# First layer of a two-layer decoder trunk: x read by features for twelve of sixteen tiles, and the fourth gate block of head 0 moved into the first pass

## The chip, the cores and the metric

The kernel runs on one core of a Trainium2 chip. A time is the device time of one launch in microseconds (us). The kernel before takes 2194.3 us, the median of three runs (2192.89 to 2194.66). PE is the matrix engine, DVE the vector engine, ACT the scalar engine, POOL the GpSimd engine, SP the engine that issues most of the DMAs (transfers between device memory and the on-chip memory, SBUF). Products are summed in PSUM, eight banks of 128 x 512 float32.

## The reference, cut to what matters

```python
# D_MODEL 2048, SEQ 512, 2 layers; layer 0: retention (8 heads), layer 1: latent attention
c_act = jax.nn.silu(c)
for i in range(DEPTH):
    mod = (c_act @ ada_w[i] + ada_b[i])[:, None, :]
    shift, scale, gate = jnp.split(mod, 3, axis=-1)
    h = rmsnorm(x, norm_g[i]) * (1.0 + scale) + shift
    ...
    x = x + gate * y
return rmsnorm(x, final_norm_g)

def retention_branch(h, pos, w_in, gn_g, w_out):
    proj = h @ w_in                       # 2048 -> 12288 columns
    q, k, v, g = jnp.split(proj, [RET_QK, 2 * RET_QK, 2 * RET_QK + RET_WIDTH], axis=-1)
    q, k = rope(q), rope(k) * (RET_DK ** -0.5)
    y = groupnorm(chunkwise_retention(q, k, v)) * gn_g
    return (jax.nn.silu(g) * y) @ w_out
```

All is in float32. rmsnorm divides every token (row of x) by its root mean square: one factor per token.

## The kernel before, in words

**Arithmetic.** A float32 operand is split in a high part (rounded to the type that PE multiplies quickly) and a low part (the rest), and a product is three products: high by high, high by low, low by high. ACT casts the high part, DVE subtracts to get the low part.

**Layout.** h is needed by features: 16 tiles hT of 128 features by 512 tokens. x is read by tokens into eight tiles `xs`. `transpose` (L493) turns one feature tile with four 128-wide matmuls against diagonals that hold the token factors, so that x is transposed and normalised at once, into a PSUM bank of the tag `aux`; ACT copies it to `xT` (L502). Six tiles are turned at the start, ten later among the products. `make_first` (L363) takes a finished tile to h: two DVE instructions write one column of shift (`b_col`, L366) and of scale (`a_col`, L367), then ACT writes hT's high half (L243) and a full copy (L245), and DVE subtracts the low half (L246).

**Modulation.** Shift and scale of 128 features need 2 x 1 MB of ada_w (`aw`, four buffers), each multiplied and summed along its rows by one DVE instruction of 2048 elements (`sum_mod`, L353).

**First pass.** The first stage works in eight units of two feature tiles (`for u in range(1, NU)`; unit 0 is written out). As a feature tile of h becomes ready, it is multiplied with three sets of weights of head 0: qk (four 128-row blocks in four PSUM banks `acc`), v (four) and g (three blocks, 384 columns, in three `aux` banks; the transposes use the fourth). qk and v share the four acc banks: `swap` (L373) copies the sums of one set to SBUF (L379) and those of the other back (L383), eight ACT copies in each unit. In the order of a unit on PE: the set that is in the banks ("here", 24 products), g (18), after the swap the other set ("there", 24), and in units 1 to 4 one tile turned after "here" and one after "there".

What the engines do beside unit u is the preparation of unit u+1, `prepare_ahead` (L517) and `prepare_behind` (L535). DVE: sum, low half of the unit's second hT, low half of the "here" weights, sum, columns, sum, low half of hT, low half of g, sum, columns, low half of "there". ACT: cast of "here", hT and its copy, casts of g and "there", the eight copies, second hT. Raw weights have three buffers (`raw`), their high and low parts three each (`whi`, `wlo`); `load_unit` (L506) issues a unit's DMAs on SP. Every engine works in program order; the helper `queued` keeps each piece behind the last instruction already issued on ACT, DVE, PE and SP (not POOL).

**After the first pass.** In unit 7 DVE computes the sine and cosine tables (L257 to L277), whose input `ret_pi` is read by a DMA that ACT issues (L254); ACT takes the sines (L279, L280) and POOL stores both tables (L597). Then a list `steps` of steps (L851) follows: two steps of 24 products each for g's fourth block ("g03", L851, in the free aux bank), and for each further head eight steps of 24 products for qk, then sixteen for v and g together, which use sums and differences of hT's halves (`form_sums`, L626: six DVE additions, two ACT casts, two DVE subtractions for two feature tiles). The steps of g03 form sums 0 and 1 beside their products, the steps of head 1's qk sums 2 to 7. ACT writes the finished banks of head 0 out after the tables and after the cast of the first step's weights (`keep_rows`, L608), and head 1's qk takes over those acc banks one by one. Outputs are stored by DMAs that POOL issues (L612).

`load_residual` (L1138) reads x by features again at the end of the first layer.

Of the kernel before, what the change touches and what calls it, by code (L numbers as in the profile page):

```python
# [9 lines left out]
F32 = mybir.dt.float32  # L10
F32R = mybir.dt.float32r
I32 = mybir.dt.int32
AF = mybir.ActivationFunctionType
ALU = mybir.AluOpType
AX = mybir.AxisListType

P = 128
# [32 lines left out]
def hybrid_trunk_kernel(  # L50
# [44 lines left out]
    def big(name, dt=F32R):  # L95
        return base.tile([P, 2, T], dt, tag="big", bufs=16, name=name)
# [7 lines left out]
    def tmp(name, shape=(P, T)):  # L104
        return base.tile(list(shape), F32, tag="tmp", bufs=6, name=name)
# [4 lines left out]
    def aux(name):  # L110
        return psum.tile([P, T], F32, tag="aux", bufs=4, name=name)
# [22 lines left out]
    def split(src, hi, lo):  # L134
        ACT.copy(hi, src)  # L135
        DVE.tensor_sub(lo, src, hi.bitcast(F32))  # L136
# [16 lines left out]
    def rows(w, u, n, c0, cn):  # L153
        return w[u * n * P : (u + 1) * n * P, c0 : c0 + cn].rearrange("(k p) n -> p k n", p=P)
# [46 lines left out]
    def w_block(w, ki, b):  # L201
        return w[0][:, ki, b * P : (b + 1) * P], w[1][:, ki, b * P : (b + 1) * P]
# [4 lines left out]
    def act_row(t):  # L207
        return t[:, 0, :], t[:, 1, :]
# [89 lines left out]
    def qk_parts(h, u):  # L298
# [10 lines left out]

    first_sets = {  # L310
        "qk": (4, lambda w, kt, b: (w_block(w, kt % 2, b), act_row(hT[kt]))),
        "g": (3, lambda w, kt, b: (w_block(w, kt % 2, b), act_row(hT[kt]))),
        "v": (4, lambda w, kt, b: (act_block(hT[kt], b), w_row(w, kt % 2))),
    }
    banks = {}
# [2 lines left out]

    def first_load(kind, u):

        cn = 384 if kind == "g" else 512
        tags = (("k4b", 4), ("k4b", 4)) if kind == "g" else (("whi", 3), ("wlo", 3))
        raw = base.tile([P, 2, cn], F32, tag="raw", bufs=3, name=f"{kind}0_{u}_raw")
        c0 = {"v": 4096, "g": 8192}.get(kind)
        for dst, src in qk_parts(0, u) if kind == "qk" else [(whole, rows(w_ret_in, u, 2, c0, cn))]:
            nc.sync.dma_start(dst(raw), src)

        def prepare():
            hl = [base.tile([P, 2, cn], F32R, tag=t, bufs=n, name=f"{kind}0_{u}_{t}{i}") for i, (t, n) in enumerate(tags)]
            ACT.copy(hl[0], raw)  # L330
            loaded[kind, u] = hl
            return lambda: DVE.tensor_sub(hl[1], raw, hl[0].bitcast(F32))

        return prepare
# [28 lines left out]
    def make_first(kt):  # L363

        k1 = slice(kt, kt + 1)
        DVE.tensor_add(b_col[0][:, k1], mods[kt, 0], bias_c[0][:, k1])  # L366
        DVE.scalar_tensor_tensor(  # L367
            out=a_col[0][:, k1], in0=mods[kt, 1], scalar=bias1[:, k1], in1=norm_c[0][:, k1], op0=ALU.add, op1=ALU.mult
        )
        hT[kt] = big(f"hT_{kt}")  # L370
        return make_h(0, kt, xT[kt // 2][:, kt % 2, :], hT[kt])
# [48 lines left out]
    def queued(fn, *args):  # L420
        with behind(A_, V_, T_, S_):
            return fn(*args)


    xs = [[big(f"x_{t}_{j}", F32) for j in range(2)] for t in range(NT)]
# [7 lines left out]
    def load_first(kind, u):  # L433
        prepares[kind, u] = queued(first_load, kind, u)

    def load_mods(kt):
        for s in range(2):
            mods[kt, s] = queued(load_mod, kt, s)
# [62 lines left out]
            )  # L501
        return lambda: ACT.copy(xT[kt // 2][:, kt % 2, :], ps)  # L502

    for kt in range(6):
        queued(queued(transpose, kt))
    def load_unit(u):  # L506
        here, there = ("qk", "v") if u % 2 == 0 else ("v", "qk")
        load_first(here, u)
        load_mods(2 * u)
        load_first("g", u)  # L510
        mods[2 * u + 1, 0] = queued(load_mod, 2 * u + 1, 0)
        load_first(there, u)
        mods[2 * u + 1, 1] = queued(load_mod, 2 * u + 1, 1)

    late = {}

    def prepare_ahead(u, first=None):  # L517


        here, there = ("qk", "v") if u % 2 == 0 else ("v", "qk")  # L520
        low = queued(prepares[here, u])
        queued(sum_mod, 2 * u, 0)
        if first is not None:
            queued(first)
        queued(low)
        queued(sum_mod, 2 * u, 1)
        low = queued(make_first, 2 * u)
        queued(sum_mod, 2 * u + 1, 0)
        queued(low)
        low = queued(prepares["g", u])  # L530
        late[u] = queued(prepares[there, u])
        queued(low)
        queued(sum_mod, 2 * u + 1, 1)
# [11 lines left out]
    low = queued(make_first, 0)  # L545
    queued(sum_mod, 1, 0)
    queued(low)
    lows = [queued(prepares[kind, 0]) for kind in ("g", "qk")]
    for low in lows:
        queued(low)  # L550
    queued(sum_mod, 1, 1)
    swap(None, "v")
    queued(products, "v", 0)
    banks["g"] = [aux(f"g0_{b}") for b in range(3)]
    queued(products, "g", 0)
    queued(swap, "v", "qk")
    low = queued(make_first, 1)
    queued(products, "qk", 0)
    prepare_ahead(1, low)
    queued(products, "qk", 1)  # L560
    queued(queued(transpose, 6))
    queued(products, "g", 1)
    queued(swap, "qk", "v")
    low = prepare_behind(1)
    queued(queued(transpose, 7))
    queued(products, "v", 1)
    for u in range(1, NU):

        here, there = ("qk", "v") if u % 2 == 0 else ("v", "qk")
        more = u + 1 < NU  # L570
        ahead = [2 * u + 6, 2 * u + 7] if 2 * u + 7 < KD else []
        if more:
            load_unit(u + 1)
            prepare_ahead(u + 1, low)
        else:
            queued(low)
            for _ in range(8):
                queued(next, tables)
        for kt in (2 * u, 2 * u + 1):
            queued(products, here, kt)  # L580
        for kt in ahead[:1]:
            queued(queued(transpose, kt))
        for kt in (2 * u, 2 * u + 1):
            queued(products, "g", kt)
        if more:
            queued(swap, here, there)
            low = prepare_behind(u + 1)
        else:
            for b, ps in enumerate(banks["v"]):
                st = tmp(f"v0_st{b}")  # L590
                queued(ACT.copy, st, ps)
                POOL.dma_start(v_d[b * P : (b + 1) * P, :], st)
            queued(swap, None, "qk")
            for _ in tables:
                pass
            for n, t in enumerate(ret_tables):
                POOL.dma_start(tables_d[n * P : (n + 1) * P, :], t)  # L597
        queued(bank_products, there, u)
        for kt in ahead[1:]:
            queued(queued(transpose, kt))  # L600
    qk0, g0 = banks["qk"], banks["g"]
    l0.__exit__(None, None, None)

# [4 lines left out]
    def keep_rows(ps, dst_d, r0, name, func=AF.Identity, own=None):  # L608

        st = lpp.tile([P, T], F32, tag="st", bufs=2, name=name) if own is None else own(name)  # L610
        ACT.activation(st, ps, func)
        POOL.dma_start(dst_d[r0 : r0 + P, :], st)  # L612

    H = T // 2

    def sums_tile(n, more):
        shape = [P, 2, 2, H]
        if n < 8:  # L620
            return base.tile(shape, F32R, tag="k4", bufs=8, name=f"sums_{n}")
        if n < 12:
            return base.tile(shape, F32R, tag="k4b", bufs=4, name=f"sums_{n}")
        return more(shape, f"sums_{n}")

    def form_sums(u, acts, sums, staged, more):  # L626
        e, o = (tmp(f"h_{2 * u + i}_f") for i in range(2))
        for f, kt in ((e, 2 * u), (o, 2 * u + 1)):
            DVE.tensor_add(f, acts[kt][:, 0, :].bitcast(F32), acts[kt][:, 1, :].bitcast(F32))
        f = staged(f"sums_{u}_f")  # L630
        DVE.tensor_add(f[0][:, 0, :], e[:, H:], o[:, H:])
        DVE.tensor_sub(f[0][:, 1, :], f[0][:, 0, :], e[:, :H])
        DVE.tensor_sub(f[1][:, 0, :], e[:, :H], e[:, H:])
        DVE.tensor_sub(f[1][:, 1, :], o[:, :H], f[0][:, 1, :])
        for i in range(2):
            s = sums[2 * u + i] = sums_tile(2 * u + i, more)
            split(f[i], s[:, :, 0, :], s[:, :, 1, :])

    def form(acts, sums, n, u, b):

# [188 lines left out]
            lambda second, u: int(second and (u % 2 == 1 or (h > 4 and u > 0))),  # L829
        )  # L830

    sums1, sums2 = {}, {}
    turns1 = turns(
        ((lambda: lpp, "own_r", 3), (lambda: base, "raw", 3)),
        ((lambda: lpp, ("own_h", "own_l"), 1), *3 * ((lambda: base, ("whi", "wlo"), 3),)),
# [12 lines left out]
    def in_turn(i):  # L848
        return None if i % 2 else tmp

    steps = plain_steps(  # L851
        2, 8, lambda u: [(whole, rows(w_ret_in, u, 8, 8192 + 384, P))], P, "g03", aux, 1,
        lambda w, ki, kt, b: w_block(w, ki, b), lambda w, ki, kt, b: act_row(hT[kt]),
        lambda b, ps: keep_rows(ps, g_d, 3 * P, "g0_st3", AF.Silu), sums=lambda u: u,
    )
    for h in range(1, RH):
        if h < 6:
            steps += plain_steps(
# [279 lines left out]
    def load_residual(r, b, tag):  # L1138
        o1_res[b, r] = l1_tile(tag, 4, f"o1_xr{r}_{b}")
        kt = 4 * r + b  # L1140
        nc.sync.dma_start(o1_res[b, r], x_t[kt * P : (kt + 1) * P, :])

    def x1_out(r, b, half=None):

# [749 lines left out]
    n_prepared = prepare_for(0)  # L1894
    for b in range(4):
        queued(keep_rows, qk0[b], qk_d, b * P, f"qk0_st{b}", AF.Identity, in_turn(b))
    for b in range(3):
        queued(keep_rows, g0[b], g_d, b * P, f"g0_st{b}", AF.Silu, tmp)
    for i, step in enumerate(steps):
        if i == n_p:  # L1900
# [272 lines left out]
```

## Time and profile before

| | us |
|---|---|
| median of three runs | 2194.3 |
| the profiled execution | 2192.7 |
| its span on the core | 2190.9 |
| PE busy in the span | 2160.2 |
| DVE busy in the span | 1557.4 |
| ACT busy in the span | 1013.1 |
| POOL busy in the span | 102.5 |
| first unit's products start on PE | 26.16 |
| second unit's products start (chain of waits) | 66.09 |
| g03 starts on PE | 161.64 |
| head 1's qk starts on PE | 173.43 |

The span is from the first to the last instruction on the core, and the profiled execution took 1.8 us more than it. A row of the timeline has the start, the duration, the engine, the line of the kernel, the operation, output and inputs, shapes and a count, and in brackets how long the engine had been idle before and what ended that. A row of the windows has, for one stretch, each engine's busy time (and instructions), the clock granted to PE (1.00 is full speed), the share of the 16 DMA engines that was busy, and the GB/s that they moved.

### The profile page before, as it was taken

How to read it: one execution, taken by the hardware profiler on the slowest of the kernel's cores; microseconds unless marked ns; L12 is line 12 of the kernel's file. 1: busy time of each engine (PE TensorE's matmuls, PEld its weight loads, DVE VectorE, ACT ScalarE, POOL GpSimd, SP SyncE). 2: the span in 40 equal slices, each digit the busy share in tenths (PEclk: the TensorE clock that was granted, in tenths of full speed). 3: DMA queues.
4: the chain of work that ended last, by engine and by line, in shares of the span. 5: the costliest groups of instructions: out<-in, count | busy, mean ns of one | idle time of the engine just before them, and what ended most of it. 6: DMA issues, size and time to landing. Idle time of an engine off the chain costs nothing.

```text
span 2190.9 us, 27827 instructions
## 1 busy us (share of the span) xinstructions
PE 2160.2 (99%) x10280; PEld 1805.1 (82%) x10280; DVE 1557.4 (71%) x2345; ACT 1013.1 (46%) x1529; POOL 102.5 (5%) x178
## 2 busy tenths in 40 slices
PE   7999999999999999999999999999999999999997
PEld 5887888888888878888888888898788889888887
DVE  7878867676676788756677767667877677776545
ACT  5664434434343444434344545344444366664443
POOL 0000000000000000010000000010000000000000
PEclk9999999999999999999999999999999999999998
DMA  9965785867768678574645556453458723235323
GB/s 382 346 246 166 231 295 181 271 214 238 247 197 278 220 256 293 184 244 150 229 156 210 171 190 203 146 161 115 156 192 301 266 87 99 83 113 178 115 99 133
DMA packets 206907, 440.26 MB, mean 201 GB/s; under 512 B 19329, under 2 KB 60321, under 8 KB 202929
## 3 DMA queue, kind: packets, MB, share of 16 engines
q1 hardware_dynamic: 194560, 399.30, 54.7%
q0 software_dynamic: 11920, 38.91, 4.5%
q8 instruction: 80, 1.31, 0.2%
q14 instruction: 57, 0.47, 0.1%
q10 hardware_dynamic: 290, 0.27, 0.0%
HBM read 395.42 MB, written 43.00 MB: 200 GB/s over the span
## 4 chain that ended last, share of the span: by engine, by line
PE 81%; DVE 6%; issue 6%; ACT 3%; DMA 3%; POOL 0%; SPq 0%; POOLq 0%; DVEq 0%; ACTq 0%
PE o L1183 13%; PE qk L163 4%; PE qk L161 4%; PE qk L162 4%; PE o L2039 4%; PE x L729 2%; PE y L729 2%; PE y L730 2%; PE y L728 2%; PE x L730 2%; PE s L729 2%; PE s L730 2%; PE x L728 2%; PE s L728 2%; PE o L162 2%
## 5 line engine op out<-in xcount | busy, mean ns | idle before, releaser
L1183 PE MATMUL o<-o_h,o_whi 128*128 128x512 f32 (+1 forms) x496 | 192.2, 388 | 0.0
L1183 PE MATMUL o<-o_h,o_wlo 128*128 128x512 f32 (+1 forms) x496 | 191.4, 386 | 0.0
L1183 PE MATMUL o<-o_l,o_whi 128*128 128x512 f32 (+1 forms) x496 | 191.3, 386 | 0.0
L163 PE MATMUL qk<-hT,qk_l 128*128 128x512 f32 x448 | 174.9, 390 | 0.5 <-DVE qk_l L136 0.5
L161 PE MATMUL qk<-hT,qk_h 128*128 128x512 f32 x448 | 174.6, 390 | 0.0
L162 PE MATMUL qk<-hT,qk_h 128*128 128x512 f32 x448 | 174.4, 389 | 0.0
L136 DVE TENSOR_TENSOR o_wlo<-o_r,o_whi 128x1024 fp32r<-128x1024 f32 x61 | 74.6, 1223 | 84.1 <-ACT o_whi L135 84.1
L136 DVE TENSOR_TENSOR qk_l<-qk_r,qk_h 128x1024 fp32r<-128x1024 f32 x56 | 68.1, 1224 | 63.7 <-ACT qk_h L135 63.7
L1183 PEld LDWEIGHTS o<-o_h,o_wlo 128*128 128x128 f32 x496 | 93.2, 188 | 18.7
L1183 PEld LDWEIGHTS o<-o_l,o_whi 128*128 128x128 f32 x496 | 93.2, 188 | 18.3
L1183 PEld LDWEIGHTS o<-o_h,o_whi 128*128 128x128 f32 x496 | 93.2, 188 | 18.3
L163 PEld LDWEIGHTS qk<-hT,qk_l 128*128 128x128 f32 x448 | 84.1, 188 | 19.6 <-DVE qk_l L136 2.1
L162 PEld LDWEIGHTS qk<-hT,qk_h 128*128 128x128 f32 x448 | 84.1, 188 | 17.5
L161 PEld LDWEIGHTS qk<-hT,qk_h 128*128 128x128 f32 x448 | 84.1, 188 | 17.4
L135 ACT CAST qk_h<-qk_r 128x1024 fp32r<-128x1024 f32 x56 | 58.0, 1051 | 85.5 <-PE qk L162 62.0
L161 PE MATMUL g<-h,g_h 128*128 128x512 f32 x232 | 90.6, 390 | 0.3 <-ACT g_h L135 0.3
L162 PE MATMUL g<-h,g_h 128*128 128x512 f32 x232 | 90.3, 389 | 0.0
L885 DVE SCALAR_TENSOR_TENSOR mod<-mod,c_bm 128x1024 f32<-128x1024 f32 x64 | 78.1, 1220 | 16.6 <-DMA mod<-in_ada_t_dram 16.5
L163 PE MATMUL g<-h,g_l 128*128 128x512 f32 x232 | 89.8, 389 | 0.0
L353 DVE SCALAR_TENSOR_TENSOR aw<-aw,c_all 128x2048 f32<-128x2048 f32 (+1 forms) x34 | 73.3, 2161 | 2.8 <-DMA aw<-in_ada_t_dram 2.8
L135 ACT CAST o_whi<-o_r 128x1024 fp32r<-128x1024 f32 x61 | 63.6, 1054 | 23.5 <-issue 10.0
L136 DVE TENSOR_TENSOR o_w_lo<-o_w_raw,o_w_hi 128x1024 fp32r<-128x1024 f32 x32 | 39.0, 1221 | 36.7 <-ACT o_w_hi L135 36.6
(1261 smaller groups left out, 6028.4 us busy)
## 6 DMA issues: line engine op xcount, KB each, us to landing
mod<-in_ada_t_dram SPq DMA_DIRECT2D x128, 512.0 KB, 5.8
o_r<-in_ret_w_out_dram SPq DMA_DIRECT2D x64, 512.0 KB, 4.3
aw<-in_ada_t_dram SPq DMA_DIRECT2D x30, 1024.0 KB, 9.0
qk_r<-in_ret_w_in_dram SPq DMA_DIRECT2D x112, 256.0 KB, 4.1
g_r<-in_mla_w_in_dram SPq DMA_DIRECT2D x32, 512.0 KB, 4.4
o_w_raw<-in_mla_w_out_dram SPq DMA_DIRECT2D x32, 512.0 KB, 3.6
qk_d<-qk_st POOLq DMA_DIRECT2D x32, 256.0 KB, 3.7
qk_r<-qk_d SPq DMA_DIRECT2D x32, 256.0 KB, 5.8
```

The lines of the kernel that those rows point to most:

```text
L135: ACT.copy(hi, src)
L136: DVE.tensor_sub(lo, src, hi.bitcast(F32))
L161: PE.matmul(o, lhs[0], rhs[0], start=first and not seeded, stop=False, skip_group_check=seeded)
L162: PE.matmul(o, lhs[0], rhs[1], start=False, stop=False, skip_group_check=seeded)
L163: return PE.matmul(o, lhs[1], rhs[0], start=False, stop=last, skip_group_check=seeded)
L353: DVE.scalar_tensor_tensor(out=aw[:, cols], in0=aw[:, cols], scalar=1.0, in1=c_all[:, cols], op0=ALU.mult, op1=ALU.mult, accum_out=col[:, ...
L728: PE.matmul(banks[b], a[0], w[0], start=first, stop=False, skip_group_check=True)
L729: PE.matmul(banks[b], a[0], w[1], start=False, stop=False, skip_group_check=True)
L730: PE.matmul(banks[b], a[1], w[0], start=False, stop=True, skip_group_check=True)
L885: DVE.scalar_tensor_tensor(out=aw, in0=aw, scalar=1.0, in1=silu_c[j], op0=ALU.mult, op1=ALU.mult, accum_out=mc[:, j, b : b + 1],)
L1183: PE.matmul(o, w[i][:, ki, c0 + b * P : c0 + (b + 1) * P], a[j], start=first and i + j == 0, stop=last and i == 1, skip_group_check=True,)
L2039: PE.matmul(banks2[b][:, cols], w[0][i][:, 0, b * P : (b + 1) * P], o2_moving(w, u, cols)[j], start=u + i + j == 0, stop=u == KD - 1 and i ...
```

## The change

- x is stored by features as pairs of tiles, and tiles 4 to 15 are read by six DMAs of 512 KB, one in each of units 2 to 7, straight into `xT`. Tiles 0 to 3 are still turned on PE. Four more 128-wide matmuls against `ones` spread the token factors over the partitions, ACT copies them to `x_factors`, and one DVE multiplication of 128 x 1024 for each pair (`normalise`) applies them. On DVE it stands between the low half of "here" and the unit's second sum.
- g is multiplied in four blocks (512 columns, four aux banks) in the first pass: 24 products of g in each unit. The two steps g03 are gone, and the list starts with head 1's qk.
- The two columns of `make_first` are written by POOL.
- The raw weights of unit 0 lie in `big` buffers, not in `raw`.
- Sums 0 and 1 are formed in unit 7, on DVE and ACT ahead of the tables.
- `load_residual` reads the new layout of x.

```diff
     first_sets = {
-        "g": (3, lambda w, kt, b: (w_block(w, kt % 2, b), act_row(hT[kt]))),
+        "g": (4, lambda w, kt, b: (w_block(w, kt % 2, b), act_row(hT[kt]))),
...
-        cn = 384 if kind == "g" else 512
+        cn = 512
         tags = (("k4b", 4), ("k4b", 4)) if kind == "g" else (("whi", 3), ("wlo", 3))
-        raw = base.tile([P, 2, cn], F32, tag="raw", bufs=3, name=f"{kind}0_{u}_raw")
+        raw = big(f"{kind}0_{u}_raw", F32) if u == 0 else base.tile(
+            [P, 2, cn], F32, tag="raw", bufs=3, name=f"{kind}0_{u}_raw"
+        )
...
-        DVE.tensor_add(b_col[0][:, k1], mods[kt, 0], bias_c[0][:, k1])
-        DVE.scalar_tensor_tensor(
-            out=a_col[0][:, k1], in0=mods[kt, 1], scalar=bias1[:, k1], in1=norm_c[0][:, k1], op0=ALU.add, op1=ALU.mult
+        POOL.tensor_add(b_col[0][:, k1], mods[kt, 0], bias_c[0][:, k1])
+        POOL.tensor_scalar(
+            out=a_col[0][:, k1], in0=mods[kt, 1], scalar1=bias1[:, k1], scalar2=norm_c[0][:, k1], op0=ALU.add, op1=ALU.mult
         )
...
-    for kt in range(6):
+    for kt in range(4):
         queued(queued(transpose, kt))
+    x_r = aux("x_r")
+    for t in range(NT):
+        queued(PE.matmul, x_r[:, t * P : (t + 1) * P], ones, diags[t], True, True)
+    factors = tmp("x_factors")
+
+    def normalise(u):
+        DVE.tensor_mul(xT[u], xT[u], factors.unsqueeze(1).to_broadcast([P, 2, T]))
+
     def load_unit(u):
...
         load_mods(2 * u)
+        if u > 1:
+            queued(nc.sync.dma_start, xT[u], x_t[u])
         load_first("g", u)
...
         queued(low)
+        if u > 1:
+            queued(normalise, u)
         queued(sum_mod, 2 * u, 1)
...
     queued(low)
+    queued(ACT.copy, factors, x_r)
     lows = [queued(prepares[kind, 0]) for kind in ("g", "qk")]
...
-    banks["g"] = [aux(f"g0_{b}") for b in range(3)]
+    banks["g"] = [aux(f"g0_{b}") for b in range(4)]
...
-    queued(queued(transpose, 6))
...
-    queued(queued(transpose, 7))
...
-        ahead = [2 * u + 6, 2 * u + 7] if 2 * u + 7 < KD else []
...
             queued(low)
+            for n in range(2):
+                queued(form_sums, n, hT, sums1, staged0, None)
             for _ in range(8):
                 queued(next, tables)
...
-        for kt in ahead[:1]:
-            queued(queued(transpose, kt))
...
-        for kt in ahead[1:]:
-            queued(queued(transpose, kt))
...
-    steps = plain_steps(
-        2, 8, lambda u: [(whole, rows(w_ret_in, u, 8, 8192 + 384, P))], P, "g03", aux, 1,
...
-    )
+    steps = []
...
-        nc.sync.dma_start(o1_res[b, r], x_t[kt * P : (kt + 1) * P, :])
+        nc.sync.dma_start(o1_res[b, r], x_t[kt // 2, :, kt % 2, :])
...
-    for b in range(3):
+    for b in range(4):
         queued(keep_rows, g0[b], g_d, b * P, f"g0_st{b}", AF.Silu, tmp)
```

`form_sums` and `sums_tile` are moved ahead of the first pass unchanged.

More of the change, by code (lines that the diff above doesn't have):

```diff
@@ L422, in queued, with sums_tile, form_sums @@
             return fn(*args)
+    H = T // 2
+    def sums_tile(n, more):
+        shape = [P, 2, 2, H]
+        if n < 8:
+            return base.tile(shape, F32R, tag="k4", bufs=8, name=f"sums_{n}")
+        if n < 12:
+            return base.tile(shape, F32R, tag="k4b", bufs=4, name=f"sums_{n}")
+        return more(shape, f"sums_{n}")
+    def form_sums(u, acts, sums, staged, more):
+        e, o = (tmp(f"h_{2 * u + i}_f") for i in range(2))
+        for f, kt in ((e, 2 * u), (o, 2 * u + 1)):
+            DVE.tensor_add(f, acts[kt][:, 0, :].bitcast(F32), acts[kt][:, 1, :].bitcast(F32))
+        f = staged(f"sums_{u}_f")
+        DVE.tensor_add(f[0][:, 0, :], e[:, H:], o[:, H:])
+        DVE.tensor_sub(f[0][:, 1, :], f[0][:, 0, :], e[:, :H])
+        DVE.tensor_sub(f[1][:, 0, :], e[:, :H], e[:, H:])
+        DVE.tensor_sub(f[1][:, 1, :], o[:, :H], f[0][:, 1, :])
+        for i in range(2):
+            s = sums[2 * u + i] = sums_tile(2 * u + i, more)
+            split(f[i], s[:, :, 0, :], s[:, :, 1, :])
     xs = [[big(f"x_{t}_{j}", F32) for j in range(2)] for t in range(NT)]
@@ L515, in hybrid_trunk_kernel, with staged0 @@
     late = {}
+    sums1 = {}
+    def staged0(name):
+        f = l0p.tile([P, D], F32, tag="aw", bufs=4, name=name)[:, 0 : 4 * H].rearrange("p (a n) -> p a n", a=4)
+        return f[:, 0:2, :], f[:, 2:4, :]
     def prepare_ahead(u, first=None):
@@ L612, in keep_rows @@
         POOL.dma_start(dst_d[r0 : r0 + P, :], st)
[L616 to L637, printed above, removed]
     def form(acts, sums, n, u, b):
@@ L830, in heads_steps @@
         )
-    sums1, sums2 = {}, {}
+    sums2 = {}
     turns1 = turns(
@@ L849, in in_turn @@
         return None if i % 2 else tmp
-    steps = plain_steps(
-        2, 8, lambda u: [(whole, rows(w_ret_in, u, 8, 8192 + 384, P))], P, "g03", aux, 1,
-        lambda w, ki, kt, b: w_block(w, ki, b), lambda w, ki, kt, b: act_row(hT[kt]),
-        lambda b, ps: keep_rows(ps, g_d, 3 * P, "g0_st3", AF.Silu), sums=lambda u: u,
-    )
+    steps = []
     for h in range(1, RH):
@@ L2152 @@
     named += [("const_rot_dram", rot), ("const_decay_dram", dec)]
-    named += [("in_x_t_dram", _np.ascontiguousarray(inputs["x"][0].T))]
+    named += [("in_x_t_dram", _np.ascontiguousarray(inputs["x"][0].T.reshape(KD // 2, 2, P, T).transpose(0, 2, 1, 3)))]
     named += [("in_ada_t_dram", _np.ascontiguousarray(_np.swapaxes(inputs["ada_w"], 1, 2)))]
```

## The prediction

> **What bounds the kernel now.** First the page, then the windows, the chain of waits in order of time, and each engine's timeline.
>
> ```profile
> PE 2160.2 (99%) x10280; PEld 1805.1 (82%) x10280; DVE 1557.4 (71%) x2345; ACT 1013.1 (46%) x1529; POOL 102.5 (5%) x178
> ```
>
> PE is the bound of the whole: what the change takes from PE's program counts only where PE is also the last to be ready. So I read the first 180 us by stages.
>
> ```profile
> 30.00:40.00 10.00, 9.73 (x47) 7.70 (x45) 8.73 (x12) 3.88 (x7) 0.00 (x0) 1.00 1.03 403
> 40.00:50.00 10.00, 6.75 (x26) 5.31 (x27) 9.43 (x10) 9.60 (x17) 0.00 (x0) 0.83 1.03 405
> 100.00:110.00 10.00, 10.00 (x50) 8.35 (x49) 8.73 (x10) 6.18 (x10) 0.00 (x0) 1.00 0.86 296
> ```
>
> Up to about 58 us the DMA engines are full (share 1.03 at 405 GB/s) and PE waits once; from then on PE is full, DVE nearly so.
>
> ```profile
> 59.46 5.74 PE qk L396 x24
> 65.20 0.89 PE xT_ps L497 x8
> 66.09 5.46 PE qk L396 x24
> 72.44 4.10 PE g L396 x18
> ```
>
> 24 products take 5.45 us, 18 take 4.10, a turned tile (eight matmul records) 0.89; unit 2 starts at 66.09. A unit of 66 products and two tiles is 16.8 us; without tiles (units 5 to 7) 15.0.
>
> **What paces a unit beside PE.** Unit 6 prepares unit 7; its rows on ACT, DVE and PE, sorted by time:
>
> ```profile
> 131.90 1.06 ACT L330 CAST v_whi<-v_raw 128x1024 fp32r<-128x1024 f32 x1 [0.64 <-PE qk L396]
> 132.99 1.23 DVE L332 TENSOR_TENSOR v_wlo<-v_raw,v_whi 128x1024 fp32r<-128x1024 f32 x1 [1.00 <-ACT v_whi L330]
> 134.13 2.29 DVE L353 SCALAR_TENSOR_TENSOR aw<-aw,c_all 128x2048 f32<-128x2048 f32 x1
> 136.34 0.15 DVE L366 TENSOR_TENSOR b_col<-mc,vcol 128x1 f32<-128x1 f32 x1
> 136.72 0.82 ACT L243 ACTIVATE hT<-xT,b_col,a_col 128x512 fp32r<-128x512 f32 x1 [3.76 <-DVE a_col L367]
> 137.14 4.24 PE L396 MATMUL g<-hT,g_k4b 128*128 128x512 f32 x18
> 138.15 0.82 ACT L330 CAST g_k4b<-g_raw 128x768 fp32r<-128x768 f32 x1
> 138.88 1.05 ACT L330 CAST qk_whi<-qk_raw 128x1024 fp32r<-128x1024 f32 x1
> 140.44 0.59 ACT L383 COPY v<-part_v 128x512 f32<-128x512 f32 x1
> 141.22 0.40 PE L396 MATMUL v<-v_whi,hT 128*128 128x512 f32 x1
> ```
>
> The cast of "here" waits for PE's end of the unit before (its buffer), so the chain starts anew with each unit. The unit starts at about 131.6 (137.14 less 24 products). Chain: cast, low half, sum, columns, hT, cast of g, cast of "there", swap; its first copy ends at 141.03, 9.4 after the start, and PE, done with g at 141.2, takes over without waiting. The chain is just covered, and the tables behind the first pass are too:
>
> ```profile
> 146.25 0.69 DVE L246 TENSOR_TENSOR hT<-h_15f,hT 128x512 fp32r<-128x512 f32 x1 [2.28 <-ACT h_15f L245]
> 144.18 0.36 ACTq L254 DMA_DIRECT2D ret_pi<-in_positions_dram  x1
> 148.31 0.43 DVE L257 CAST ret_sin<-ret_pi 128x512 f32<-128x512 int32 x1 [1.37 <-DMA ret_pi<-in_positions_dram]
> 158.74 0.63 ACT L279 ACTIVATE ret_sin<-ret_sin 128x512 f32<-128x512 f32 x1 [3.00 <-DVE ret_cos L277]
> 159.90 1.04 ACT L135 CAST g_h<-g_r 128x1024 fp32r<-128x1024 f32 x1
> 161.64 0.39 PE L161 MATMUL g<-hT,g_h 128*128 128x512 f32 x1
> 163.02 1.58 ACT L611 ACTIVATE qk_st<-qk 128x512 f32<-128x512 f32 x3 [1.60 <-DMA tables_d<-ret_cos]
> 164.47 1.60 ACT L611 ACTIVATE g_st<-g 128x512 f32<-128x512 f32 x3
> 165.91 1.09 ACT L135 CAST g_h<-g_r 128x1024 fp32r<-128x1024 f32 x1
> 168.18 1.29 DVE L629 TENSOR_TENSOR h_f<-hT 128x512 f32<-128x512 f32 x2
> 170.63 0.43 DVE L634 TENSOR_TENSOR sums_f<-h_f,sums_f 128x256 f32<-128x256 f32 x1
> 171.28 1.29 DVE L136 TENSOR_TENSOR sums<-sums_f,sums 128x512 fp32r<-128x512 f32 x2 [0.23 <-ACT sums L135]
> 173.43 0.39 PE L161 MATMUL qk<-hT,qk_h 128*128 128x512 f32 x1
> 178.96 1.23 DVE L136 TENSOR_TENSOR qk_l<-qk_r,qk_h 128x1024 fp32r<-128x1024 f32 x1 [0.66 <-ACT qk_h L135]
> ```
>
> Unit 7 starts at 146.7 (141.22 plus 5.45) and ends at 161.64. ACT is held by the sines until 159.90 and by the store of the tables until 163.02. PE does not mind: g03 needs neither an acc bank nor those copies, and fills 161.64 to 173.43.
>
> **The change part by part.** PE's own program: twelve tiles less, 12 x 0.89 = 10.7, eight records for the factors more, 0.9; g's 48 products only move. Alone that is -9.8 us. What becomes of it:
>
> (a) *Up to unit 2.* Two raw g blocks grow by 131 KB each, 0.26 MB or 0.65 us at 405 GB/s, ahead of a cast that waits for its DMA:
>
> ```profile
> 41.62 1.05 ACT L330 CAST qk_whi<-qk_raw 128x1024 fp32r<-128x1024 f32 x1 [0.18 <-DMA qk_raw<-in_ret_w_in_dram]
> 43.20 2.07 PE L497 MATMUL xT_ps<-x_diag,x 128*128 128x128 f32 x8 [3.47 <-ACT xT L502]
> ```
>
> The two turned tiles that stood there go (2.07 and 0.89), six products of g come (1.4), and ACT loses a 0.5 us copy behind the cast. At the start hT's first cast falls behind three other ACT pieces in the built order (some 2.3 us), which the 3.47 us of waiting absorb. Unit 2's load is 0.65 MB larger (1.6 us), which its own waits partly show. I take unit 2 at 66.5, +0.4; bounds -1 (loads not later) and +5.7 (two holds as in (b), 2.3 each, beside 1.1).
>
> (b) *Units 2 to 6.* PE's part is 72 products, 16.4 us, against 16.8 or 15.0. The chain grows. `normalise` is one two-input DVE instruction of 1024, 1.14 from the row at 132.99 to the next. The g cast takes 0.23 more (1.05 against 0.82). Then the columns on POOL: before, hT starts 0.38 after the sum's end (136.34). No row shows POOL adding one column; a memset of one column takes 0.10, a power of one column 0.56:
>
> ```profile
> L2149 POOL MEMSET const-float32-0.0<- 128x1 f32 x1 | 0.1, 99 | 0.2 <-issue 0.2
> L131 POOL TENSOR_TENSOR x_r<-x_v,mhalf 128x1 f32<-128x1 f32 x4 | 2.2, 562 | 10.9 <-DVE x_v L129 10.9
> L131 POOL TENSOR_TENSOR gn_r<-gn_v,mhalf 128x4 f32<-128x4 f32 x8 | 8.1, 1015 | 374.0 <-DVE gn_v L129 374.0
> L131 POOL TENSOR_TENSOR kv_r_r<-kv_r_v,mhalf 128x4 f32<-128x4 f32 x1 | 1.9, 1915 | 4.1 <-DVE kv_r_v L129 4.1
> 1657.10 1.22 DVE L885 SCALAR_TENSOR_TENSOR mod<-mod,c_k4b 128x1024 f32<-128x1024 f32 x1
> 1657.28 1.94 POOL L131 TENSOR_TENSOR q_r_r<-q_r_v,mhalf 128x4 f32<-128x4 f32 x1 [75.98 <-DVE q_r_v L129]
> ```
>
> I take 0.4, nearer to the power. The last rows matter more. The same four-column power takes 1.01 eight times, but 1.94 and 1.92 where DVE had just begun a SCALAR_TENSOR_TENSOR with two inputs in SBUF: it ends 0.9 to 1.0 after that instruction's end (1658.32), as if it began there. In the changed order the scale column is released by a sum, and DVE's next instruction is the next sum, of the same kind, 2.21 long, with its data already there. So POOL is held for that sum: hT starts 2.21 + 0.4 + 0.05 = 2.7 after the sum, 2.3 later than before. (With nothing held it would be 0.1 to 0.3 later.) The shift column is not on the path, nor the second scale column, which ACT's copies cover.
>
> [...]
>
> The chain is then 9.4 + 1.14 + 0.23 + 2.3 = 13.1 against 10.9 of products ahead of the swap. PE waits 2.2 us in each unit, and a unit takes 13.1 + 5.45 + 0.15 = 18.7. Five units are 93.5 against 80.6 (66.09 to 146.7): **+12.9**. Without the hold the chain is about 11.0, a unit 16.5, and the five +1.9. DMAs are no bound at this pace: 6.3 MB in 18.7 us are 337 GB/s, under the 405 shown.
>
> (c) *Unit 7 to the steps of head 1's qk.* Counting from unit 7's start: hT's last low half ends at +0.2. Sums 0 and 1 now stand ahead of the tables on DVE, 4.3 each (168.18 to 172.5), and their casts ahead of ret_pi's DMA on ACT. The fourth cast is released at 4.5 + 2.9 = +7.4; the DMA goes then, arrives 4.1 later (144.18 to 148.31), the tables take 10.4 (to 158.74): sines at +22.0. Behind these on ACT come the cast of head 1's first weights, +23.2 (1.16 after the sines' start), the first copy of a qk bank, +24.1, the other three at +26.3 (163.02, 4.3 after the sines' start), four of g to +29.7, and the second weights' cast, so that their low half starts at +30.8. PE is through with unit 7 at +16.4 and waits until +24.7 for a bank: the 10.9 us that g03 took go into this wait. Before, that low half starts at 178.96, +32.3. From there sums, casts and products stand in one order in both: **-1.5**, of which I give 0.5 back for PE's clock, which the window 40 to 50 shows at 0.83 after 3.5 us of waiting. So -1.0; bounds -1.6 (no loss) and +1 (clock lost for longer).
>
> The larger g tiles on DVE (0.27 a unit), the saved tile copies on ACT and load_residual's layout (rows of 2 KB as before) are off these chains: 0, and if the first's cover went, 2 us in all.
>
> Sum: +0.4 + 12.9 - 1.0 = **+12.3**. The profiled execution of before took 2192.7 (span 2190.9 and 1.8), 1.6 under the median of 2194.3; 2205.0 on it is 2206.6 on the median.
>
> **Rivals.** *POOL is not held* (it reads its column in a gap, or DVE's next sum waits for its DMA as at the start): +0.4 + 1.9 - 1.0 = +1.3, 2195.6. For it: only two rows show the hold. Against: DVE has no gaps there. *PE stays the bound* (faster): the point is the place of ret_pi and of the sines on ACT. Were ret_pi's DMA issued ahead of the casts and the first weights cast ahead of the sines, PE would run on at +16.4, and if POOL were also not held the whole 9.8 would be kept: 2184.5. Against: both engines work in program order, and the built order has them as in (c). *PE also loses its clock in each wait*: the trace shows the loss after a wait of 3.5 us, and has no row for one of 2.2. About 1.6 us a unit and five units: +8, 2214.6. [...]
>
> **Chances.** Forecast 0.66 (2200 to 2211: the hold missing in one or two units, or two more at the start); not held 0.17 (2193 to 2198); PE's clock too 0.10; PE the bound 0.05; the change not doing what it says, for x read by features late, 0.02 (DMA again the bound, some 2203). The range 2194 to 2214 leaves out most of the third, the fourth and a part of the second. This kernel's runs differ by 0.1%, so 0.2% (4.4 us) is what can be told from no change: faster 0.05, same 0.18, slower 0.77.
>
> **What would show it.** In the new profile: POOL's a_col at 2.3 to 2.7 us rather than 0.4; ACT's hT waiting for POOL and PE's first product of "there" for ACT's copy, 2 us in each of units 2 to 6; unit starts 18.7 apart; the sines 22 after unit 7's start, and PE waiting 8 us for qk_st ahead of head 1's qk. POOL rows of 0.6 or less, with units 16.5 apart, would prove (b) wrong; a qk that starts before the sines, (c).

## The result, and the profile after

The changed kernel takes **2212.35 us** (median of four, 2210.5 to 2213.3), the kernel before on the same chip 2194.48. The ratio is 1.0082, with a 95% interval from 1.0064 to 1.0099: slower by 0.8%, 17.9 us, where 12.3 were forecast. The profiled execution has a span of 2208.7 against 2190.9, and the first line of its page reads:

```profile
PE 2159.7 (98%) x10192; PEld 1802.5 (82%) x10192; DVE 1560.8 (71%) x2317; ACT 1006.0 (46%) x1516; POOL 140.7 (6%) x210
```

PE has 88 records less, 9.8 us of work by the forecast's count, and is as busy as before (2160.2): some 9.3 us went into running slowly (the mean granted clock is 0.992 against 0.997), and PE's idle time has grown by 18.3 us (49.0 against 30.7). POOL's busy time has grown by 38 us, for 32 columns. PE's timeline shows where PE waits; in brackets stand the length and the releaser.

```profile
62.84 0.50 PE L398 MATMUL qk<-hT,qk_whi 128*128 128x512 f32 x1 [2.32 <-ACT qk L385]
...
73.86 5.60 PE L398 MATMUL g<-hT,g_k4b 128*128 128x512 f32 x24
81.80 0.50 PE L398 MATMUL v<-v_whi,hT 128*128 128x512 f32 x1 [2.34 <-ACT v L385]
...
101.89 0.50 PE L398 MATMUL qk<-hT,qk_whi 128*128 128x512 f32 x1 [1.83 <-ACT qk L385]
...
121.96 0.50 PE L398 MATMUL v<-v_whi,hT 128*128 128x512 f32 x1 [1.83 <-ACT v L385]
...
140.91 0.79 PE L398 MATMUL qk<-hT,qk_whi 128*128 128x512 f32 x1 [2.33 <-ACT qk L385]
...
160.93 0.50 PE L398 MATMUL v<-v_whi,hT 128*128 128x512 f32 x1 [1.83 <-ACT v L385]
...
173.55 5.60 PE L398 MATMUL g<-hT,g_k4b 128*128 128x512 f32 x24
...
190.30 0.79 PE L161 MATMUL qk<-hT,qk_h 128*128 128x512 f32 x1 [5.70 <-ACT qk_st L653]
...
236.39 0.39 PE L745 MATMUL z<-vg_00o_h,hT 128*128 128x512 f32 x1
```

PE waits once in each of units 1 to 6 for ACT's copies of the swap, and once ahead of head 1's qk. A unit's start is the start of its g less 24 products (5.45): unit 2 starts at 68.4, unit 7 at 168.1. The first product of head 1's v and g, at 236.39, stood in the kernel before at

```profile
218.59 0.39 PE L728 MATMUL z<-vg_00o_h,hT 128*128 128x512 f32 x1
```

so the whole 17.8 us is there by then, and nothing is gained or lost behind it. The chain of waits from unit 2 on names the pieces (start, duration, what):

```profile
71.36 1.22 DVE xT L541
72.57 2.22 DVE aw L355 x2
...
74.89 2.32 POOL a_col L369
...
77.96 0.80 ACT h_6f L245
78.76 0.94 ACT g_k4b L332
79.70 0.94 ACT qk_whi L332
80.64 0.49 ACT part_qk L381
...
81.16 0.60 ACT v L385
...
81.80 7.40 PE v L398 x24
...
89.22 1.06 ACT qk_whi L332
...
121.03 2.30 DVE aw L355 x2
...
123.43 3.38 POOL a_col L369
...
127.55 0.80 ACT h_11f L245
128.35 0.95 ACT qk_whi L332
...
130.47 1.22 DVE xT L541
```

Read it as the forecast's chain: `normalise` (L541), sum, **POOL's column for 2.3 us**, hT, casts, swap, PE. Two things in it were not in the forecast. PE's 24 products take 7.40 there, not the 5.60 that g's 24 take above. And from 109 to 141 PE is not in the chain at all: DVE, POOL's other column (3.38) and ACT make a loop that feeds itself.

Why POOL takes so long is seen where its rows stand between DVE's (timeline, sorted by time):

```profile
64.13 1.22 DVE L334 TENSOR_TENSOR v_wlo<-v_raw,v_whi 128x1024 fp32r<-128x1024 f32 x1
64.31 3.37 POOL L369 TENSOR_SCALAR a_col<-mc,bias,vcol 128x1 f32<-128x1 f32 x1 [5.83 <-DVE aw L355]
65.27 2.28 DVE L355 SCALAR_TENSOR_TENSOR aw<-aw,c_all 128x2048 f32<-128x2048 f32 x1
67.48 0.08 DVE L355 DVE_READ_ACCUMULATOR aw<-aw,c_all 128x1 f32 x1
67.64 0.19 POOL L368 TENSOR_TENSOR b_col<-mc,vcol 128x1 f32<-128x1 f32 x1
```

The column begins at 64.31, just behind the start of a low half on DVE, and ends at 67.68, just behind the end of the sum that follows (67.56). It did not get in between the two instructions. With DVE idle the next column, b_col, takes 0.19.

### The profile page after: what moved, and what is told of

It reads as the page before. It is cut to its first block, busy times and chain, and to the rows that moved or that the text cites. A ratio compares the mean times of both kernels' runs of the same rounds, so it can differ in the third digit from the quotient of the medians.

```text
span 2208.7 us, 27660 instructions
## 1 busy us (share of the span) xinstructions
PE 2159.7 (98%) x10192; PEld 1802.5 (82%) x10192; DVE 1560.8 (71%) x2317; ACT 1006.0 (46%) x1516; POOL 140.7 (6%) x210
## 4 chain that ended last, share of the span: by engine, by line
PE 80%; DVE 8%; issue 4%; ACT 3%; DMA 3%; POOL 1%; SPq 0%; DVEq 0%; POOLq 0%; ACTq 0%
PE o L1196 13%; PE qk L161 4%; PE qk L162 4%; PE qk L163 4%; PE o L2052 4%; PE x L746 2%; PE y L746 2%; PE y L747 2%; PE y L745 2%; PE x L747 2%; PE s L746 2%; PE s L747 2%; PE x L745 2%; PE s L745 2%; PE o L163 2%
## 5 line engine op out<-in xcount | busy, mean ns | idle before, releaser
L1196 PEld LDWEIGHTS o<-o_h,o_whi 128*128 128x128 f32 x496 | 93.2, 188 | 18.2
L1196 PEld LDWEIGHTS o<-o_l,o_whi 128*128 128x128 f32 x496 | 93.2, 188 | 18.2
L163 PEld LDWEIGHTS qk<-hT,qk_l 128*128 128x128 f32 x448 | 84.6, 189 | 17.9 <-DVE qk_l L136 0.3
L135 ACT CAST qk_h<-qk_r 128x1024 fp32r<-128x1024 f32 x56 | 57.9, 1050 | 85.9 <-PE qk L162 66.5
```

Of the source, the lines that this page charges most:

```text
L163: return PE.matmul(o, lhs[1], rhs[0], start=False, stop=last, skip_group_check=seeded)
L1196: PE.matmul(o, w[i][:, ki, c0 + b * P : c0 + (b + 1) * P], a[j], start=first and i + j == 0, stop=last and i == 1, skip_group_check=True,)
```

## The experiments

Each time is a median. The kernel before took 2192.4 to 2193.1 on the same chip in these runs; differences are to that, and the changed kernel stands at +17.9 in this count. The expectations of e1 to e4 and of e6 are absolute times that start from the changed kernel's 2212.35 and the 2194.48 beside it; I compare them as differences too.

**e1: the columns on DVE again.** The rest of the change stays.

```diff
-        POOL.tensor_add(b_col[0][:, k1], mods[kt, 0], bias_c[0][:, k1])
-        POOL.tensor_scalar(out=a_col[0][:, k1], in0=mods[kt, 1], scalar1=..., scalar2=..., op0=ALU.add, op1=ALU.mult)
+        DVE.tensor_add(b_col[0][:, k1], mods[kt, 0], bias_c[0][:, k1])
+        DVE.scalar_tensor_tensor(out=a_col[0][:, k1], in0=mods[kt, 1], scalar=..., in1=..., op0=ALU.add, op1=ALU.mult)
```

> The changed kernel with the two columns of make_first on DVE again; all else of the change stays. Theory A (POOL's scale column is shut out while DVE's sums run one behind the other, and the chain of a unit is 2.3 us longer for it): with the column on DVE the chain is 13.1 - 2.3 = 10.8 us against 10.9 of products, so units 2 to 6 come 16.4 to 16.6 us apart, unit 7 starts at about 149 instead of 168, PE still waits some 8 us ahead of head 1's qk, and the time is about 2194.5 (2192 to 2197). Rival B (the longer unit is the work that was added to DVE, normalise and the larger g tile, and POOL's column costs only its own 0.3 us): units stay 18.5 to 20 us apart, 2209 to 2211.

Measured: 2191.28, -1.3, ratio to before 0.9993 (0.9984 to 1.0003): the time of before, and 19.2 us under the changed kernel; A's range is -2.5 to +2.5 as a difference. PE's timeline of e1:

```profile
71.83 5.61 PE L398 MATMUL g<-hT,g_k4b 128*128 128x512 f32 x24
...
88.16 5.61 PE L398 MATMUL g<-hT,g_k4b 128*128 128x512 f32 x24
...
172.20 0.80 PE L161 MATMUL qk<-hT,qk_h 128*128 128x512 f32 x1 [7.65 <-ACT qk_st L653]
```

The units are 16.33 apart, which is 72 products and nothing else; PE waits in none of them. So `normalise` and the larger g tile are covered (B falls), and POOL's column, with what follows from it, is the whole loss of the first pass. The wait ahead of head 1's qk is 7.65, near the forecast's 8.3.

**e2: sums 0 and 1 out of unit 7** (columns still on POOL).

```diff
-            for n in range(2):
-                queued(form_sums, n, hT, sums1, staged0, None)
...
-                sums=lambda u, h=h: {0: 2, 1: 3, 3: 4, 4: 5, 6: 6, 7: 7}.get(u) if h == 1 else None,
+                sums=lambda u, h=h: u if h == 1 else None,
```

> The changed kernel with sums 0 and 1 taken out of unit 7: head 1's qk forms one sum in each of its eight steps. Theory A (the wait of 5.7 us ahead of head 1's qk comes from the sums that stand ahead of the tables on DVE and ahead of the DMA of the positions on ACT): units 2 to 6 stay 19 to 20 us apart, unit 7 starts at 168 as before this edit, the sines come 12 to 13 us after it, PE waits less than 1 us ahead of head 1's qk and loses no clock there (5.7 and some 2 us), and DVE is then the bound of the qk steps, some 0.3 us in each (2.3 in all): 2205 to 2208. Rival C (what PE waits for there is regained in any case, since DVE's low halves of head 1's weights set the end of qk): 2211 to 2213.

Measured: 2207.15, +14.5, ratio to before 1.0063 (1.0048 to 1.0078); 3.4 us under the changed kernel, less than the 4.4 to 7.4 that A's range makes. PE no longer waits ahead of head 1's qk, but it waits later, ahead of the first product of v and g:

```profile
232.31 0.74 PE L743 MATMUL z<-vg_00o_h,hT 128*128 128x512 f32 x2 [2.30 <-ACT vg_00o_h L777]
```

C falls, yet part of the wait has only moved: a step with a sum takes DVE 5.72 us, against 5.45 of products. In the profiled run the stretch from unit 7's start to this product takes 63.2 us, against 68.3 in the changed kernel, but the first pass before it is 1.0 longer (unit 7 starts at 169.1), with five stretches of half clock where the changed kernel has four.

**e3: both edits.**

> Both edits: the columns on DVE, and sums 0 and 1 in the steps of head 1's qk. Theory A (the two losses are independent, and what is left of the change are twelve turned tiles less on PE): e1's time less 5.7 to 10 us for the wait and its clock, more 2.3 for DVE in the qk steps: 2187 (2184 to 2190), faster than the kernel before by 0.2 to 0.5%. Rival D (normalise alone makes the chain of a unit too long, so that the tiles saved on PE bring nothing even without the two losses): 2193 to 2196.

Measured: 2189.02, -3.6, ratio to before 0.9983 (0.9973 to 0.9992): faster than before, but 0.9 short of A's range as a difference (-10.5 to -4.5); D (-1.5 to +1.5) falls. Of e1's 7.65 us of waiting only 2.3 came out as time: PE waits 2.28 and 1.86 us again at 211.83 and 217.09, ahead of products of v and g. That DVE is the bound there is argued so far; e9 tests it.

**e4: the kernel before with nothing changed but the columns on POOL** (e1's edit the other way round).

> The kernel before with one edit: the two columns of make_first on POOL. Theory A (hold): the chain of a unit is 9.4 + 2.3 = 11.7 us against 10.45 of products and a turned tile in units 1 to 4 and 9.55 in units 5 and 6, so PE waits 1.2 to 2.1 us in each: +9 us, 2203 (2200 to 2208 with half clock after some of the waits); a_col takes 2.3 and 3.4 us on POOL where DVE goes on with the next sum. Rival B (POOL's column costs its own 0.3 us): 2194 to 2196.

Measured: 2209.97, ratio to before 1.0078 (1.0060 to 1.0096). This one edit costs 17.4 us, as much as the whole change, and more than either theory gave. PE waits 1.8 to 2.3 us in each of units 1 to 6, but the units are up to 20.6 us apart, where A's chain with the turned tile makes 18.2: PE's granted clock is 0.91 in the four stretches of 20 us from 80 to 160, which e6 takes up. There are four stretches of half clock in the units; at 1.7 us each, an estimate from the changed kernel's rows, they and A's 9 us make 15.9.

**e5: DVE waits for POOL, not POOL for DVE.** One DVE instruction more behind each pair of columns.

```diff
         POOL.tensor_scalar(out=a_col[0][:, k1], ...)
+        DVE.tensor_copy(small(f"a_seen_{kt}"), a_col[0][:, k1])
```

> The changed kernel (columns on POOL) with one DVE instruction more behind each pair of columns: it copies one column of a_col, so DVE waits for POOL there and begins its next sum only when POOL has the column. Theory A (POOL's 2.3 and 3.4 us are time in which DVE's next instructions shut it out; by itself the column takes 0.34 us): a_col takes 0.34 us in every row, each pair costs DVE 0.6 to 0.9 us of waiting, units are 16.4 to 17.0 us apart instead of 19 to 20, and the time is that of the columns on DVE (2191.3) plus 0 to 4 us: 2191 to 2195, 17 us or more faster than the changed kernel although an instruction and a wait were added. Rival E (POOL is slow for another reason, such as its own queue or the semaphore): a_col still takes 2.3 us, DVE's added wait makes it worse, 2215 or more.

Measured: 2191.91, -0.5, ratio to before 0.9999 (0.9990 to 1.0008): 18.4 us under the changed kernel by *adding* a wait. The groups of POOL's instructions (busy, mean ns of one, idle before), first of the changed kernel:

```profile
L369 POOL TENSOR_SCALAR a_col<-mc,bias,vcol 128x1 f32<-128x1 f32 x15 | 34.0, 2268 | 90.4 <-DVE aw L355 90.4
```

of e4:

```profile
L367 POOL TENSOR_SCALAR a_col<-mc,bias,vcol 128x1 f32<-128x1 f32 x15 | 33.9, 2258 | 90.2 <-DVE aw L353 90.2
```

and of e5:

```profile
L369 POOL TENSOR_SCALAR a_col<-mc,bias,vcol 128x1 f32<-128x1 f32 x15 | 5.1, 341 | 62.0 <-DVE aw L355 62.0
```

The same instruction takes 341 ns when DVE stands still and 2268 when DVE goes on with the next sum. E falls; that DVE's run shuts this column out is shown. The added copy costs DVE a wait of 0.48 and 0.15 of its own, as its timeline shows:

```profile
105.67 0.15 DVE L372 COPY a_seen<-a_col 128x1 f32<-128x1 f32 x1 [0.48 <-POOL a_col L369]
```

In the changed kernel two DVE instructions one behind the other shut the scale column out for both (3.37, the row at 64.31). That is not so for every column. In e5 the shift column b_col, which takes 0.19 with DVE idle, is let in between two such instructions; it ends at 75.74, with the second one under way:

```profile
75.00 0.69 DVE L246 TENSOR_TENSOR hT<-h_6f,hT 128x512 fp32r<-128x512 f32 x1
75.17 0.57 POOL L368 TENSOR_TENSOR b_col<-mc,vcol 128x1 f32<-128x1 f32 x1 [2.50 <-DVE aw L355]
75.60 1.22 DVE L334 TENSOR_TENSOR g_k4b<-g_raw,g_k4b 128x1024 fp32r<-128x1024 f32 x1
```

What decides between the two is not shown.

**e6: PE kept busy in the changed kernel's waits.**

```diff
+    zeros = base.tile([P, 32], F32R, name="zeros")
+    DVE.tensor_scalar(out=zeros, in0=ones[:, :32], scalar1=0.0, scalar2=None, op0=ALU.mult)
...
+    def fill(u):
+        for _ in range(10):
+            PE.matmul(banks["g"][3][:32, :], zeros, hT[2 * u][:, 0, :], start=False, stop=False, skip_group_check=True)
...
         if more:
+            queued(fill, u)
             queued(swap, here, there)
```

> The changed kernel with ten products more in each of units 1 to 6, ahead of the swap: a 128x32 tile of zeros times hT, added to the fourth bank of g, so that PE is busy for 2.3 us while it would wait for the swap; nothing else changes. Theory F (PE's waits of 1.8 to 2.3 us cost half clock for 3.4 us behind some of them; of five units three or four lose 1.1 to 1.7 us so): no row of the first pass at half clock, units 2 to 6 all 18.95 us apart, unit 7 starts 4 to 5 us earlier, 2207.5 to 2209. Rival G (the half clock is not what makes units 20 us long, or products of zeros do not hold the clock): 2211 to 2214.

Measured: 2205.82, +13.4, ratio to before 1.0064 (1.0047 to 1.0081): 4.5 us under the changed kernel with 60 products more, within the 3.4 to 4.9 of F's range. Unit 7 starts 6.3 us earlier, at 161.8, and 1.6 of that go into a longer wait ahead of head 1's qk (7.28 against 5.70). Windows of the changed kernel (PE's busy time is in the second column, its granted clock the third number from the end):

```profile
84.00:86.00 2.00, 2.00 (x6) 1.52 (x6) 2.00 (x2) 1.41 (x3) 2.00 (x1) 0.50 1.00 418
...
122.00:124.00 2.00, 2.00 (x9) 1.65 (x10) 2.00 (x3) 1.91 (x4) 0.57 (x1) 1.00 0.86 268
142.00:144.00 2.00, 2.00 (x6) 1.58 (x5) 2.00 (x4) 1.87 (x5) 1.62 (x1) 0.50 1.01 393
```

and one of e6, ten times as long:

```profile
80.00:100.00 20.00, 20.00 (x89) 15.36 (x88) 16.00 (x15) 11.45 (x18) 5.98 (x4) 1.00 0.88 336
```

In the changed kernel the clock is 0.50 behind some of the waits and 1.00 behind others; in e6 no stretch from 60 us to the end of the first pass is below 1.00, and units 2 to 6 take 18.6 to 19.0. G falls. These are almost the forecast's 18.7, and +13.4 is almost its +12.3: what the forecast had left out is, for the most part, the half clock.

**e7: e3 with sum 0 in unit 7 beside the DMA of the positions, the other sums one step earlier. e8: e7 with ACT's copies of g's banks behind the cast of the second qk weights.**

```diff
+            queued(next, tables)
+            queued(form_sums, 0, hT, sums1, staged0, None)
-            for _ in range(8):
+            for _ in range(7):
                 queued(next, tables)
...
-                sums=lambda u, h=h: u if h == 1 else None,
+                sums=lambda u, h=h: u + 1 if h == 1 and u < 7 else None,
```

> e3 (columns on DVE, no sums ahead of the tables) with sum 0 in unit 7 while the DMA of the positions is under way (the DMA ahead of it on ACT), and sums 1 to 7 in steps 0 to 6 of head 1's qk. Theory A (from unit 7 to head 1's v and g DVE is the bound: tables 10.4 us, then 5.72 us for each qk step with a sum against 5.45 of products): 3 of the 4.3 us of sum 0 lie in the time in which DVE waited for the positions, and no sum is left in front of the first weights of v and g, where PE waits 2.3 and 1.9 us in e3: 2184 to 2187. Rival H (PE's waits there come from ACT's copies of the banks alone): 2188 to 2190.

e8 beside that:

```diff
-    for b in range(4):
-        queued(keep_rows, g0[b], g_d, b * P, f"g0_st{b}", AF.Silu, tmp)
     for i, step in enumerate(steps):
...
         n_prepared += prepare_for(i + 1)
+        if i == 0:
+            for b in range(4):
+                queued(keep_rows, g0[b], g_d, b * P, f"g0_st{b}", AF.Silu, tmp)
```

> e7 with the four copies of g's banks behind the cast of the second qk weights on ACT instead of ahead of it, so that DVE's second low half and all that follows start up to 2 us earlier. Theory A: PE's wait at the second qk step goes and DVE has a lead of some 2 us over the qk steps: 1 to 3 us faster than e7, 2182 to 2186. Rival H (ACT is not late there): as e7 within 0.5.

Measured: e7 2188.88 (-3.5, ratio 0.9986, 0.9976 to 0.9995), e8 2187.58 (-4.8, ratio 0.9978, 0.9969 to 0.9988). Both miss what A gave: e7 can't be told from e3 and lies in H's range, and e8 lies between its A and its H. In e8 PE is through with head 1's qk some 8 us earlier than before, at 210.45, and then waits for a bank that ACT has not copied: on ACT the copies stand behind the casts of the first weights of v and g, and these wait for DVE, which forms sum 7 first:

```profile
213.25 0.74 PE L745 MATMUL x<-vg_00e_h,hT 128*128 128x512 f32 x1 [2.80 <-ACT qk_st L653]
```

The products behind it are recorded with 0.63 each instead of 0.39, half clock again. So the 8 us were there, and nearly half was given back at once.

**e9: e8 with sum 7 in the fifth step of v and g.**

```diff
-                sums=lambda u, h=h: u + 1 if h == 1 and u < 7 else None,
+                sums=lambda u, h=h: u + 1 if h == 1 and u < 6 else None,
...
+    steps[12].sums = 7
```

> e8 with sum 7 formed in the fifth step of v and g (its first use is in the eighth) instead of in step 6 of head 1's qk, so that DVE prepares the first weights of v and g 4.3 us earlier. Theory A (DVE, not PE, ends the stretch from unit 7 to v and g: in e8 PE ends qk at 210.3 and then waits 2.8 us, with half clock for 3.4 us behind it): the wait and the half clock go, 4 us: 2183.5 (2182 to 2185), nearly all of the 9.8 us that the change takes from PE's program. Rival H (ACT's copies of the banks, which stand behind its casts, hold PE in any case): within 1 us of e8's 2187.6.

Measured: 2184.79, -8.3, ratio to before 0.9960 (0.9947 to 0.9974): the fastest of all, as A gave; H falls. PE's timeline, where qk ends and v and g begin:

```profile
211.18 0.39 PE L163 MATMUL qk<-hT,qk_l 128*128 128x512 f32 x1
211.41 0.39 PE L745 MATMUL x<-vg_00e_h,hT 128*128 128x512 f32 x1
```

No wait is left there, and 7.2 of the 7.3 us of span won stand at this point (218.59 before).

## Why the prediction was right in direction and short in size

| step | forecast | measured |
|---|---|---|
| (a) up to unit 2 | +0.4, start 66.5 | +2.3, start 68.4 |
| (b) units 2 to 6 | +12.9, 18.7 each | +19.1, 19.9 each |
| (c) unit 7 to head 1's v and g | -1.0 | -3.6 |
| sum | +12.3 | +17.8 |

The direction and the mechanism held. The size did not: 2212.35 lies above the 2200 to 2211 that had most of the chance, and it stayed inside the outer range (to 2214) partly by luck, since (a) and (b) together were 8.1 short and (c) came out 2.6 better.

**(a)** Its sum was right for a kernel without the hold (in e1, without POOL's columns, unit 2 starts at 66.4, against 66.5 forecast; its parts were not measured one by one), but it left out the hold as a term. The other 2 us are the hold in the unit before (2.46 at 55.79 on POOL's timeline), which the forecast had only in its bounds.

**(b)** The mechanism stands as forecast: POOL held for the next sum (2.32 against the 2.61 that 2.21 + 0.4 make; that a sum would hold POOL for its whole 2.21 was an estimate, since the rows of before show 0.9 us lost behind an instruction of 1.22), the swap late, PE waiting 1.8 to 2.3 us in every unit. The cover and what uncovers it were right too: e1 puts `normalise` and the g cast at nothing once the hold is gone. The step that failed is its last, "a unit takes 13.1 + 5.45 + 0.15 = 18.7". From a unit's start to PE's first product behind the swap it took 12.9 to 13.4 in the five units, where 13.1 and 0.15 were forecast, but the 5.45 behind it (from start to start) was 7.1 to 7.2 in four of them, because PE's granted clock was 0.50 for 3.41 us behind the wait; in the fifth it was 5.6. That is the rival "PE also loses its clock in each wait", held at 0.10; e6 shows that it was true beside the forecast, not instead of it. Its price, 8, was near to the 6.2 by which (b) was short; its 1.6 a unit was an estimate without a row of such a wait, and 3.41 us at 0.50 make 1.7 here, behind four of the six. The trace of before shows a lower clock behind a wait of 3.47 us; here one of 1.83 was enough.

A smaller part of (b) was put wrongly: the prediction kept the second scale column off the path and let the cast of "here" always start with PE's end of the unit before. That column is held over two DVE instructions (3.37), and where PE is at full clock it is on the path: the loop of DVE, POOL and ACT takes 18.96 by itself (from `normalise` at 111.51 to the next at 130.47).

**(c)** The order was as forecast. The changed kernel's timelines of ACT and DVE:

```profile
173.93 0.36 ACTq L254 DMA_DIRECT2D ret_pi<-in_positions_dram  x1
177.15 0.43 DVE L257 CAST ret_sin<-ret_pi 128x512 f32<-128x512 int32 x1 [1.75 <-DMA ret_pi<-in_positions_dram]
187.58 0.63 ACT L279 ACTIVATE ret_sin<-ret_sin 128x512 f32<-128x512 f32 x1 [8.98 <-DVE ret_cos L277]
189.66 0.59 ACT L653 ACTIVATE qk_st<-qk 128x512 f32<-128x512 f32 x1
196.29 1.23 DVE L136 TENSOR_TENSOR qk_l<-qk_r,qk_h 128x1024 fp32r<-128x1024 f32 x1 [5.28 <-ACT qk_h L135]
```

The DMA goes 5.8 after unit 7's start (7.4 forecast), its data are there 3.2 later (4.1), the sines start at 19.5 (22.0), PE waits 5.7 (8.3), and the second low half starts at 28.2 (30.8). The 2.6 us too many have two causes: unit 7's start was late by the half clock, which DVE and ACT did not share (some 1.5: hT's last low half ends at 166.78, 1.3 before unit 7's start, not 0.2 behind it), and the DMA was 0.9 quicker.

**Not held and PE the bound** (0.17 and 0.05) did not happen in the changed kernel, but e1 is the first and e9 is near the second (it also moves the sums), and they give -1.3 and -8.3 where the prediction had +1.3 and -9.8. Of the -9.8 counted for PE alone, e9 realises 8.3. What stands in its way without POOL's hold is DVE: g03's 10.9 us of products had been the cover of two sums, and with that cover moved away DVE, not PE, ends the stretch from unit 7 to head 1's v and g (e3, e7, e8); e9, with one sum moved out of it, loses the wait.

## What to carry to other kernels

Before a small instruction is moved to POOL to relieve DVE, look at what DVE does next: behind it, a run of DVE instructions with two inputs each made a 0.34 us column 2.3 to 3.4 us long here, and if a chain goes through it, one wait of DVE for POOL was cheaper than the hold (e5: 0.48 of waiting and 0.15 for the copy, and 18.4 us less in all). Products that look out of place may be the cover of another engine's work; when they are moved, that work must move too. And a wait of PE of two microseconds has to be priced with the clock that it may cost behind it, here some 1.7 us more in four cases of six (half of 3.41 us at a granted clock of 0.50, an estimate).

## What the runs showed of the hardware that had not been expected

PE ran at half clock behind waits far shorter than the 3.5 us that the trace of before shows (granted clock 0.50 in both). Of the six waits of 1.83 to 2.34 us in the changed kernel's units four were followed by 3.4 us at a granted clock of 0.50, two (at 62.84 and 121.96) by none; the length does not separate them (1.83 is in both groups, and so is 2.3). The trace's windows, cut where the clock changes, show what goes with it (PE's busy time, then the granted clock as the third number from the end):

```profile
99.94:103.35 3.41, 1.58 (x7) 1.24 (x7) 3.41 (x4) 3.28 (x6) 0.00 (x0) 1.00 0.57 172
103.35:106.76 3.41, 3.41 (x9) 2.64 (x8) 3.25 (x3) 2.12 (x4) 3.40 (x2) 0.50 1.00 399
120.42:123.83 3.41, 1.87 (x8) 1.57 (x9) 3.41 (x4) 3.25 (x7) 0.40 (x1) 1.00 0.87 311
```

The four stretches at half clock begin at 82.87, 103.35, 140.90 and 161.38, and each lasts 3.41; the beginnings are 20.48, 37.55 and 20.48 apart, 6, 11 and 6 times 3.413. So they lie on one grid in this trace, and in its waits the half clock goes with how long PE was idle within one stretch of that grid. The wait that ends at 101.89 lies in one stretch whole and leaves PE 1.58 us of work there: the next stretch is at half clock. The equally long one that ends at 121.96 lies across two stretches, with 1.87 us of work in the second: no half clock follows. The same holds for the eighteen such waits of the changed kernel, e2 and e4 (worked out from the PE rows for e2 and e4): all thirteen stretches at half clock follow one in which PE was busy for 1.07 to 1.58 us, and with 1.67 to 2.13 none follows. The line near 1.6 is not sharp: with 1.55 (58.98 to 62.39, the wait that ends at 62.84) none followed either. In e4 the grid lies otherwise (a stretch at half clock begins at about 81.03, by its rows at 80.75 and 81.37). No run moved a wait against the grid with all else kept. Products of zeros kept the clock up as well as others (e6: 1.00 in every stretch of 20 us from 60 to 180).
